# Delta net in a two-layer mixer block: decay columns spread by two rounded products, backward direction reversed by its reads

## The chip, the cores and the metric

The kernel runs on one core of a Trainium2 chip. The metric is the device time of one execution in microseconds (us); lower is better. TensorE (PE) does the matrix products, its weight loads are shown apart as PEld; VectorE (DVE), ScalarE (ACT) and GpSimd (POOL) do the elementwise work; SyncE (SP) issues most of the transfers.

## The reference

Two layers over 256 latent and 256 context tokens of width 1024. Each layer is a half-step SwiGLU, then four token mixers side by side (a convolution, a linear recurrence, a gated delta net in both directions, windowed attention), merged by sigmoid gates, an output product and a second SwiGLU. The change touches the delta net alone:

```python
def gdn_chunked(q, k, v, beta, g, s0):
    ...
    gc = jnp.cumsum(g, axis=-1)
    decay = jnp.exp(jnp.where(tril, gc[..., :, None] - gc[..., None, :], -jnp.inf))
    ...
def gdn_branch(qkv, qkv_c, z, z_c, a, a_c, b, b_c, p, ctx_out):
    for d in range(2):
        fl = _flip if d else _ident
        ...
        oc, s_ctx = gdn_direction(fl(qkv_c), ...)
        ol, _ = gdn_direction(fl(qkv), ..., s_ctx, *prm)
        o_lat.append(fl(ol))
        o_ctx.append(fl(oc))
    y = _gdn_out(o_lat[0] + o_lat[1], z, p['gdn_norm_g'])
    y_c = _gdn_out(o_ctx[0] + o_ctx[1], z_c, p['gdn_norm_g']) if ctx_out else None
```

There are 4 heads of 128 channels. The second layer needs no context output.

## The kernel before

Activations lie transposed in SBUF, weights stream in from HBM as `wr` or `raw`. The dense products are fp32 quantities split into two rounded (float32r) parts: ACT casts the high part (L123), DVE or POOL subtracts to get the low part (L124), and three products at L427, L428 and L429 add up high by high, high by low and low by high.

The delta net works on 16 chunks of 32 tokens in each direction; a partition row of 128 holds 4 heads by 32 tokens. For each layer its parts are:

- `gdn_scalars` computes the gates of both directions. The running sums come out of a product into `pg`, and L718 copies them to `gc` (a column of 128 values for each direction and chunk). L720 makes their negative `ngc`, L722 to L727 further factors. L817 turns two of these into tables.
- `gdn_decay` runs 8 times in a layer, each time for one direction and 4 chunks. L739 puts a constant mask (`capr`) into a bank of PSUM; L742 adds, chunk by chunk, the column of `gc` spread over 128 columns: the column is the stationary operand, broadcast, and the fp32 identity moves. An fp32 product is two instructions on PE, so a call has 8 of them at L742. ACT takes the exponential at L746 with `ngc` as the bias.
- the scan over the chunks: L923, L935 and L940 are its products, ACT (L942) and DVE (L943) finish the output of a step, and L945 stores every second step to `ospill` in DRAM. Both directions run in the same step; the backward one is stored in the order in which it is computed.
- `gdn_out` runs once for 128 tokens: 4 times in layer 0, twice in layer 1. It reads the backward part `o1`, the forward part `ot` (both L1009) and the gate `sz` (L1011); four fp32 products at L1014 with the constant `J` reverse the 32 tokens of each group of `o1`; L1016 adds, L1019 squares with a sum on ACT, L1021 and L1023 (a power on POOL) give the norm, L1025 applies it, L1028 transposes on PE, L1032 multiplies by the gate, and the split into rounded parts (L159, L161) gives the operand of the merges.

The streams of a layer (delta net, scan, `gdn_out`, merges, convolution, and the dense products that fill in between) are generators. A string per layer sets in which order they are stepped; the instruction scheduler then orders each engine's instructions by a simulated timeline, so that an edit can move instructions far from it. Each engine works off its instructions in the order that this gives, waiting on semaphores.

Of the kernel before, what the change touches and what calls it, by code (L numbers as in the profile page):

```python
# [12 lines left out]
F32 = mybir.dt.float32  # L13
F32R = mybir.dt.float32r
BF16 = mybir.dt.bfloat16
AF = mybir.ActivationFunctionType
ALU = mybir.AluOpType
P = 128
# [34 lines left out]
class Net:  # L53
# [609 lines left out]
    def gdn_scalars(self, l, H):  # L663
        nc = self.nc
# [32 lines left out]
        V.tensor_add(z3, A, self.vec[:, V_DT:V_DT + 2].unsqueeze(2).to_broadcast([P, 2, N_CH]))  # L697
        g = self.softplus(zz, 32, self.small(128, "gsp", 1))
        na = self.small(2, "na", 1)
# [17 lines left out]
        gc = self.small(64, "gc", 1)  # L717
        V.tensor_copy(gc, pg[:, :64])  # L718
        ngc = self.small(32, "ngc", 1)
        V.tensor_scalar(ngc, gc[:, :32], -1.0, None, op0=ALU.mult)  # L720
# [6 lines left out]
        nc.scalar.activation(kst, kst, AF.Exp)  # L727
        self.gs = dict(g=g, ngc=ngc, beta=be, gc=gc[:, :32], cd=cd.rearrange("p (n h) -> p n h", h=4), egc=eg, kst=kst)

# [5 lines left out]
    def gdn_decay(self, d, g, dec):  # L735
        nc = self.nc
        o = d * N_CH + 4 * g
        pr = self.ps("pg")
        nc.tensor.matmul(pr.rearrange("p (n c) -> p n c", n=4), self.identr,  # L739
                         self.capr.unsqueeze(1).to_broadcast([P, 4, P]), start=True, stop=False)  # L740
        for i in range(4):
            nc.tensor.matmul(pr[:, i * P:(i + 1) * P], self.gs["gc"][:, o + i:o + i + 1].to_broadcast([P, P]),  # L742
                             self.ident, start=False, stop=i == 3)
        for i in range(4):
            s = slice(i * P, (i + 1) * P)
            nc.scalar.activation(dec[:, s], pr[:, s], AF.Exp, bias=self.gs["ngc"][:, o + i:o + i + 1])  # L746
# [203 lines left out]
    def gdn_init(self):  # L950
        nc = self.nc
        dr = lambda n, s: self.dr.tile(s, F32, tag=n, bufs=1, name=n)
        self.gc_t = self.sb.tile([P, 776], F32, tag="R", bufs=2, name="gcst")
        nc.sync.dma_start(self.gc_t, self.t["gcst"])
        self.capr = self.sb.tile([P, P], F32R, tag="capr", bufs=1, name="capr")
        nc.scalar.copy(self.capr, self.gcst("cap"))
        self.gsp = dr("gsp", [8, P, 2, 3, 256])
        self.asp, self.ospill = (dr(n, [8, P, 2, 256]) for n in ("asp", "ospill"))
        self.ascr = dr("ascr", [2, P, 2048])
        self.rscr = dr("rscr", [P, 1024])  # L960
        self.szspill = dr("szspill", [P, 4, 512])
# [41 lines left out]
    def gdn_out(self, go, y):  # L1003
# [3 lines left out]
        tok = slice(go * P, (go + 1) * P)  # L1007
        for x, d, g in ((o1, 1, (1 - go) if go < 2 else (5 - go)), (ot, 0, go)):
            nc.sync.dma_start(x.rearrange("p (q c) -> p q c", q=2),  # L1009
                              self.ospill[2 * g:2 * g + 2, :, d].rearrange("q p c -> p q c"))  # L1010
        nc.sync.dma_start(sz.rearrange("p (h t) -> p h t", h=4), self.szspill[:, :, tok])  # L1011
        pj = self.ps("pg")
        for i in range(4):
            nc.tensor.matmul(pj[:, (3 - i) * P:(4 - i) * P], self.gcst("J"), o1[:, i * P:(i + 1) * P],  # L1014
                             start=True, stop=True)
        V.tensor_add(ot, pj, ot)  # L1016
        sq = self.small(4, "osq", 1)
        for i in range(4):
            nc.scalar.activation(pj[:, i * P:(i + 1) * P], ot[:, i * P:(i + 1) * P], AF.Square,  # L1019
                                 accum_out=sq[:, i:i + 1])  # L1020
# [600 lines left out]
```

## Time and profile before

| | |
|---|---|
| median of 3 runs | 2763.76 us (2760.72 to 2766.8) |
| profiled execution, its own time | 2763.57 us |
| its span on the core | 2761.8 us |
| granted TensorE clock, mean | 0.972 of full speed |
| PE busy | 2595.2 us (94%) |
| DVE busy | 1914.8 us (69%) |
| ACT busy | 1157.0 us (42%) |
| POOL busy | 716.5 us (26%) |

The span is what the profiler shows between the first and the last instruction; times such as "2445" are microseconds from its start. Layer 0's mixers lie at about 500 to 1060 us, layer 1's at about 2080 to 2470 us. A line like L742 is line 742 of the kernel before; the changed kernel's lines are some 3 or 4 higher from there on.

### The profile page before, as it was taken

Reading aid. Unit: us, or ns where it says so; the run is one execution under the profiler, and the core shown is the slowest. Engines: PE = TensorE matmul, PEld = TensorE weight load, DVE = VectorE, ACT = ScalarE, POOL = GpSimd, SP = SyncE. Lnnn points to the kernel's source line nnn. Section 1 sums busy time; section 2 is a strip of 40 time slices with the busy share of each in tenths; the row PEclk is TensorE's granted clock in tenths of the full one; section 3 lists DMA queues with packets and bytes.
Section 4 is the critical chain, followed back from the end, with each engine's and each line's share of the span. In section 5 each row is a group of like instructions: output and inputs, shape, how many; then the busy total and the mean of one; then the engine's idle time right before and its main releaser. Section 6 shows DMA issues by size and latency. Waiting matters only on the chain.

```text
span 2761.8 us, 38864 instructions
## 1 busy us (share of the span) xinstructions
PE 2595.2 (94%) x14534; PEld 2169.7 (79%) x14534; DVE 1914.8 (69%) x3261; ACT 1157.0 (42%) x2240; POOL 716.5 (26%) x497
## 2 busy tenths in 40 slices
PE   7999999998998999999999989999999988988998
PEld 4877778777777787878778887888897977877897
DVE  4795966678889734266979565748567899756455
ACT  3222245473454533353322353332444546545443
POOL 1323223223111334443233333332310011111221
PEclk9999999999999999999999999999999999999999
DMA  7554633245323434438865448965364764457353
GB/s 269 197 212 153 211 122 105 62 138 166 106 85 98 137 117 126 160 107 288 317 210 186 135 153 302 321 211 194 101 243 151 242 190 136 131 165 262 124 183 107
DMA packets 194779, 477.80 MB, mean 173 GB/s; under 512 B 32816, under 2 KB 72976, under 8 KB 192544
## 3 DMA queue, kind: packets, MB, share of 16 engines
q1 hardware_dynamic: 173216, 424.39, 46.6%
q10 hardware_dynamic: 15264, 30.95, 3.2%
q0 software_dynamic: 6112, 19.99, 1.8%
q8 instruction: 114, 1.87, 0.3%
q14 instruction: 73, 0.60, 0.1%
HBM read 401.82 MB, written 73.45 MB: 172 GB/s over the span
## 4 chain that ended last, share of the span: by engine, by line
PE 50%; DVE 13%; DMA 6%; ACT 4%; issue 3%; POOL 1%; SPq 0%; ACTq 0%; DVEq 0%; POOLq 0%
PE pm L427 13%; PE pm L429 13%; PE pm L428 13%; DMA C<-in_win_dram 2%; DVE C L1157 2%; DVE wl L124 2%; PE pg L923 1%; DVE junk L203 1%; DMA wr<-in_f_dram 1%; DVE lru L1099 1%; DMA wr<-in_wo_dram 1%; DVE G L913 1%; PE px L1297 1%; PE pg L428 1%; PE pg L427 1%
## 5 line engine op out<-in xcount | busy, mean ns | idle before, releaser
L427 PE MATMUL pm<-h,wh 128*128 128x512 f32 (+1 forms) x2512 | 897.5, 359 | 31.8 <-ACT h L159 9.8
L429 PE MATMUL pm<-h,wl 128*128 128x512 f32 (+1 forms) x2512 | 895.2, 357 | 10.0 <-DVE wl L124 9.9
L428 PE MATMUL pm<-h,wh 128*128 128x512 f32 (+1 forms) x2512 | 896.8, 357 | 5.6 <-POOL h L161 5.5
L123 ACT CAST wh<-wr 128x1024 fp32r<-128x1024 f32 x304 | 318.2, 1047 | 618.8 <-DMA wr<-in_f_dram 210.2
L427 PEld LDWEIGHTS pm<-h,wh 128*128 128x128 f32 x2512 | 480.8, 192 | 111.9 <-ACT h L159 12.1
L429 PEld LDWEIGHTS pm<-h,wl 128*128 128x128 f32 x2512 | 480.5, 191 | 88.2 <-DVE wl L124 15.1
L428 PEld LDWEIGHTS pm<-h,wh 128*128 128x128 f32 x2512 | 481.0, 192 | 77.9 <-POOL h L161 7.5
L124 POOL TENSOR_TENSOR wl<-wr,wh 128x1024 fp32r<-128x1024 f32 x108 | 279.8, 2591 | 605.6 <-ACT wh L123 593.9
L124 DVE TENSOR_TENSOR wl<-wr,wh 128x1024 fp32r<-128x1024 f32 x196 | 269.3, 1375 | 215.8 <-ACT wh L123 215.0
L203 DVE SCALAR_TENSOR_TENSOR junk<-wa,cb 128x1024 bf16<-128x1024 f32 x256 | 364.3, 1462 | 9.0 <-DMA wa<-in_adaw_dram 3.9
L161 POOL TENSOR_TENSOR F<-G,F 128x512 fp32r<-128x512 f32 (+1 forms) x94 | 139.1, 1479 | 356.4 <-ACT F L159 341.9
L1157 DVE SCALAR_TENSOR_TENSOR C<-C,vec 128x482 f32<-128x482 f32 (+29 forms) x240 | 162.7, 678 | 4.4 <-ACT C L1149 1.4
L427 PE MATMUL pm<-wh,F 128*128 128x512 f32 x368 | 144.4, 396 | 7.7 <-DVE G L441 3.9
L428 PE MATMUL pm<-wl,F 128*128 128x512 f32 x368 | 144.2, 392 | 0.0
L429 PE MATMUL pm<-wh,F 128*128 128x512 f32 x368 | 143.4, 392 | 0.0
L124 DVE TENSOR_TENSOR wl<-raw,wh 128x1024 fp32r<-128x1024 f32 x62 | 76.3, 1232 | 65.9 <-ACT wh L123 65.9
L140 DVE TENSOR_TENSOR T<-C,T 128x512 fp32r<-128x512 f32 x76 | 68.3, 902 | 68.1 <-ACT T L138 64.8
L919 ACT ACTIVATE wk<-wk,cd 128x128 f32<-128x128 f32 x224 | 75.2, 392 | 87.3 <-PE pg L940 49.2
L441 DVE TENSOR_TENSOR G<-G,pm 128x512 f32<-128x512 f32 (+1 forms) x93 | 54.4, 585 | 79.9 <-PE pm L429 76.5
L159 ACT CAST F<-G 128x512 fp32r<-128x512 f32 (+1 forms) x94 | 50.9, 541 | 135.4 <-DVE G L441 135.3
L123 ACT CAST wh<-raw 128x1024 fp32r<-128x1024 f32 x64 | 67.0, 1049 | 89.7 <-PE pm L428 42.7
L620 DVE SCALAR_TENSOR_TENSOR G<-pm,vec,G 128x506 f32<-128x506 f32 (+5 forms) x126 | 87.2, 692 | 21.9 <-ACT G L615 20.2
(408 smaller groups left out, 4399.9 us busy)
## 6 DMA issues: line engine op xcount, KB each, us to landing
wr<-in_f_dram SPq DMA_DIRECT2D x204, 512.0 KB, 4.3
wa<-in_adaw_dram SPq DMA_DIRECT2D x64, 1024.0 KB, 5.1
wr<-in_win_dram SPq DMA_DIRECT2D x94, 512.0 KB, 3.6
raw<-in_f_dram SPq DMA_DIRECT2D x30, 1024.0 KB, 5.0
C<-in_win_dram SPq DMA_DIRECT2D x76, 256.0 KB, 5.0
pre<-T ACTq DMA_DIRECT2D x76, 256.0 KB, 4.9
pre<-T POOLq DMA_DIRECT2D x76, 256.0 KB, 5.7
wl<-pre SPq DMA_DIRECT2D x36, 512.0 KB, 5.3
```

What stands on the lines that cost most here:

```text
L123: nc.scalar.copy(h, r)
L124: (nc.gpsimd if pool_lo else nc.vector).tensor_sub(l, r, h.bitcast(F32))
L140: nc.vector.tensor_sub(lo, raw, h.bitcast(F32))
L161: eng.tensor_sub(lo, src, hi.bitcast(F32))
L203: nc.vector.scalar_tensor_tensor(junk, w3[:, a], 1.0, self.cb[:, s], op0=ALU.mult, op1=ALU.mult, accum_out=self.modT[l][:, i + a, s:s + 1])
L427: nc.tensor.matmul(ps, wh, xh, start=first, stop=False)
L428: nc.tensor.matmul(ps, wh, xl, start=False, stop=False)
L429: nc.tensor.matmul(ps, wl, xh, start=False, stop=last)
L441: nc.vector.tensor_mul(hf[:, c], sg[:, c], pu[:, c])
L620: nc.vector.scalar_tensor_tensor(acc[:, :, d:], src[:, :, :n - d], w(j), acc[:, :, d:], op0=ALU.mult, op1=ALU.add)
L919: nc.scalar.activation(S(d, n + 1)[:, hc], S(d, n)[:, hc], AF.Copy, scale=gs["cd"][:, d * N_CH + n, h:h + 1])
L1157: V.scalar_tensor_tensor(o, x, w(j), o, op0=ALU.mult, op1=ALU.add)
```

## The change

In `gdn_scalars` two rounded columns are made from `gc`: `gcr[0]` is its rounded copy (ACT), `gcr[1]` the rounded rest (DVE). `gdn_decay` spreads both, with the rounded identity moving: eight rounded products for four fp32 ones. In `gdn_out` the backward part is read by four transfers, each of 32 tokens of 4 heads, with the rows of each group in reverse; the products with `J` are gone, the add reads `o1` from SBUF, and the squares are written there. A small workspace of `softplus` moves into the tile of constants.

```diff
-        g = self.softplus(zz, 32, self.small(128, "gsp", 1))
+        g = self.softplus(zz, 32, self.gc_t[:, 776:904])
...
         V.tensor_copy(gc, pg[:, :64])
+        gcr = [self.sb.tile([P, 32], F32R, tag=f"gcr{e}", bufs=1, name="gcr") for e in range(2)]
+        nc.scalar.copy(gcr[0], gc[:, :32])
+        V.tensor_sub(gcr[1], gc[:, :32], gcr[0].bitcast(F32))
...
         for i in range(4):
-            nc.tensor.matmul(pr[:, i * P:(i + 1) * P], self.gs["gc"][:, o + i:o + i + 1].to_broadcast([P, P]),
-                             self.ident, start=False, stop=i == 3)
+            for gc in self.gs["gcr"]:
+                nc.tensor.matmul(pr[:, i * P:(i + 1) * P], gc[:, o + i:o + i + 1].to_broadcast([P, P]),
+                                 self.identr, start=False, stop=i == 3 and gc is self.gs["gcr"][1])
...
-        self.gc_t = self.sb.tile([P, 776], F32, tag="R", bufs=2, name="gcst")
-        nc.sync.dma_start(self.gc_t, self.t["gcst"])
+        self.gc_t = self.sb.tile([P, 904], F32, tag="R", bufs=2, name="gcst")
+        nc.sync.dma_start(self.gc_t[:, :776], self.t["gcst"])
...
-        for x, d, g in ((o1, 1, (1 - go) if go < 2 else (5 - go)), (ot, 0, go)):
-            nc.sync.dma_start(x.rearrange("p (q c) -> p q c", q=2),
-                              self.ospill[2 * g:2 * g + 2, :, d].rearrange("q p c -> p q c"))
+        nc.sync.dma_start(ot.rearrange("p (q c) -> p q c", q=2),
+                          self.ospill[2 * go:2 * go + 2, :, 0].rearrange("q p c -> p q c"))
+        g = (1 - go) if go < 2 else (5 - go)
+        for i in range(4):
+            nc.sync.dma_start(o1[:, i * P:(i + 1) * P],
+                              self.ospill[2 * g + 1 - i // 2, :, 1, (1 - i % 2) * P:(2 - i % 2) * P]
+                              .rearrange("(h t) c -> h t c", h=4)[:, ::-1])
         nc.sync.dma_start(sz.rearrange("p (h t) -> p h t", h=4), self.szspill[:, :, tok])
-        pj = self.ps("pg")
-        for i in range(4):
-            nc.tensor.matmul(pj[:, (3 - i) * P:(4 - i) * P], self.gcst("J"), o1[:, i * P:(i + 1) * P],
-                             start=True, stop=True)
-        V.tensor_add(ot, pj, ot)
+        V.tensor_add(ot, o1, ot)
...
-            nc.scalar.activation(pj[:, i * P:(i + 1) * P], ot[:, i * P:(i + 1) * P], AF.Square,
+            nc.scalar.activation(o1[:, i * P:(i + 1) * P], ot[:, i * P:(i + 1) * P], AF.Square,
                                  accum_out=sq[:, i:i + 1])
```

The scheduler places the new and the old instructions as follows. First DVE in layer 0, at the end of `gdn_scalars`; `cv` and `G` are the convolution of the delta net's inputs, `mx` belongs to the attention. Before:

```order
L718 COPY gc_3824<-pg_3816 128x64 [waits PE_49]
L720 TENSOR_SCALAR ngc_3826<-gc_3824 128x32 [waits DVE_49]
L726 TENSOR_TENSOR kst_3832<-gc_3824 128x32
L658 SCALAR_TENSOR_TENSOR cv_3531<-G_3960,G_3955 128x16x32 [waits Activation_49]
L1264 TENSOR_REDUCE mx_4583<-px_4586 128x1 [waits PE_49]
L620 SCALAR_TENSOR_TENSOR G_3963<-px_3183,vec_3143,G_3963 128x2x253 [waits Activation_49,Pool_49]
L817 TENSOR_TENSOR gcst_3475<-egc_3830,gcst_3475 128x128 [waits Activation_49]
L817 TENSOR_TENSOR gcst_3475<-kst_3832,gcst_3475 128x128 [waits Activation_49]
```

The same place of the changed kernel:

```order
L718 COPY gc_3823<-pg_3815 128x64 [waits PE_49]
L723 TENSOR_SCALAR ngc_3829<-gc_3823 128x32 [waits DVE_49]
L729 TENSOR_TENSOR kst_3835<-gc_3823 128x32
L658 SCALAR_TENSOR_TENSOR cv_3531<-G_3995,G_3990 128x16x32 [waits Activation_49]
L1268 TENSOR_REDUCE mx_4618<-px_4621 128x1 [waits PE_49]
L620 SCALAR_TENSOR_TENSOR G_3998<-px_3183,vec_3143,G_3998 128x2x253 [waits Activation_49,Pool_49]
L721 TENSOR_TENSOR gcr_3826<-gc_3823,gcr_3825 128x32 [waits Activation_49]
L821 TENSOR_TENSOR gcst_3475<-egc_3833,gcst_3475 128x128 [waits Activation_49]
```

The subtraction that makes the low column (L721) stands behind the convolution step at L620.

Then PE at the end of layer 1's mixers, from the last product of the scan to the first merge; `pm` banks are dense products (24 in a group: 8 pieces of 3 products), `y` is the output of `gdn_out`. Before:

```order
L935 MATMUL pg_19934<-vn_19932,G_19549 128x128 [waits DVE_49]
L940 MATMUL pg_19934<-wk_18669,gt_19547 32x128 x4
...
L427 MATMUL pm_21035<-h_15873,wh_21031 128x256 [waits Activation_49]
...
L1014 MATMUL pg_20796<-G_20790,gcst_16524 128x128 [waits DMAHW2_49,PE_49]
L1014 MATMUL pg_20796<-G_20790,gcst_16524 128x128 x3
...
L429 MATMUL pm_21066<-h_15873,wl_21063 128x256
L1028 MATMUL pg_20811<-ident_63,G_20791 128x128 [waits DMAHW3_49,DVE_49,PE_49]
L1028 MATMUL pg_20811<-ident_63,G_20791 128x128 x3
L1014 MATMUL pg_20890<-G_20884,gcst_16524 128x128 [waits DMAHW5_49,PE_49]
L1014 MATMUL pg_20890<-G_20884,gcst_16524 128x128 x3
L1028 MATMUL pg_20905<-ident_63,G_20885 128x128 [waits DMAHW6_49,DVE_49,Activation_49]
L427 MATMUL pg_20986<-y_20822,wh_20918 128x256 [waits PE_49,Activation_49]
```

The changed kernel from its last scan product on:

```order
L939 MATMUL pg_19996<-vn_19994,G_19611 128x128 [waits DVE_49]
L944 MATMUL pg_19996<-wk_18731,gt_19609 32x128 x4
L427 MATMUL pm_20986<-h_15900,wh_20982 128x256 [waits Activation_49]
...
L427 MATMUL pm_21017<-h_15900,wh_21013 128x256 [waits Activation_49]
...
L427 MATMUL pm_21093<-h_15900,wh_21089 128x256 [waits Activation_49]
...
L427 MATMUL pm_21124<-h_15900,wh_21120 128x256 [waits Activation_49]
L428 MATMUL pm_21124<-h_15901,wh_21120 128x256
L1032 MATMUL pg_20871<-ident_63,G_20853 128x128 [waits DMAHW5_49,DVE_49,PE_49]
L1032 MATMUL pg_20871<-ident_63,G_20853 128x128 x3
...
L1032 MATMUL pg_20963<-ident_63,G_20945 128x128 [waits DMAHW4_49,DVE_49,PE_49]
L1032 MATMUL pg_20963<-ident_63,G_20945 128x128 x3
L427 MATMUL pg_21044<-y_20882,wh_20976 128x256 [waits PE_49,Activation_49]
```

Four groups of 24 dense products now stand between the last scan product and the merges, where there were 2 products left of one group and two groups more; the second transposes no longer have products of `gdn_out` ahead of them.

At the same place DVE's order in the changed kernel (only `gdn_out`'s own instructions):

```order
L1020 TENSOR_TENSOR G_20853<-G_20852,G_20853 128x512 [waits DMAHW6_49,DMAHW7_49,DMAHW2_49,DMAHW1_49]
L1025 TENSOR_SCALAR osq_20862<-osq_20862 128x4 [waits Activation_49]
L1029 TENSOR_TENSOR G_20853<-G_20853,orr_20868 128x512 [waits Pool_49]
L1020 TENSOR_TENSOR G_20945<-G_20944,G_20945 128x512 [waits DMAHW6_49,DMAHW5_49,DMAHW7_49,DMAHW4_49,DMAHW0_49]
...
L1036 SCALAR_TENSOR_TENSOR G_20852<-pg_20871,vec_16232,G_20854 128x128 [waits DMAHW3_49,PE_49]
```

The second call's add (the second L1020) stands directly behind the first call's L1029, and waits for transfers alone.

## Rows read from the trace of the kernel before

**Rows 1.** The page: busy time of each engine, share of the span, instructions.

```profile
PE 2595.2 (94%) x14534; PEld 2169.7 (79%) x14534; DVE 1914.8 (69%) x3261; ACT 1157.0 (42%) x2240; POOL 716.5 (26%) x497
```

**Rows 2.** Busy time by stretch: length, PE, PEld, DVE, ACT, POOL, clock, DMA.

```profile
524.00:531.00 7.00, 7.00 (x53) 6.42 (x52) 6.83 (x15) 5.76 (x19) 2.36 (x1) 1.00 0.24 75
531.00:540.00 9.00, 6.61 (x45) 5.42 (x44) 6.63 (x16) 9.00 (x36) 0.00 (x0) 1.00 0.01 2
960.00:1060.00 100.00, 98.00 (x477) 79.29 (x475) 47.98 (x82) 41.69 (x82) 40.53 (x26) 1.00 0.41 126
2084.00:2460.00 376.00, 337.98 (x2587) 295.64 (x2586) 304.93 (x688) 205.44 (x523) 36.56 (x32) 0.96 0.54 171
2445.00:2460.00 15.00, 7.12 (x52) 6.82 (x53) 8.29 (x17) 5.82 (x20) 2.04 (x2) 0.88 0.44 143
```

**Rows 3.** Instructions by line, PE and PEld: busy us, mean (or min/median/max) ns.

```profile
L742 PEld LDWEIGHTS pg<-ident,gc x128: 185/190/192, 524.4 to 2113.2; 128*128 128x128 f32 x128
...
L428 PEld LDWEIGHTS pm<-h,wh 128*128 128x128 f32 x2512 | 481.0, 192 | 77.9 <-POOL h L161 7.5
...
L1014 PE MATMUL pg<-G,gcst 128*128 128x128 f32 x48 | 6.9, 276 | 1.7 <-DMA G<-ospill 1.7
...
L389 PE MATMUL px<-T 128*128 128x2 f32 x32 | 3.9, 244 | 0.8 <-DVE T L386 0.8
```

**Rows 4.** Timeline of layer 0's decay columns: start us, us, what.

```profile
524.05 2.36 POOL L124 TENSOR_TENSOR wl<-wr,wh 128x1024 fp32r<-128x1024 f32 x1 [3.61 <-PE pg L739]
...
524.37 2.07 DVE L720 TENSOR_SCALAR ngc<-gc 128x32 f32<-128x32 f32 x1
...
524.51 1.95 PE L742 MATMUL pg<-ident,gc 128*128 128x128 f32 x16
...
526.71 3.19 ACT L746 ACTIVATE dec<-pg,ngc 128x128 f32<-128x128 f32 x12
...
527.40 0.73 DVE L620 SCALAR_TENSOR_TENSOR G<-px,vec,G 128x506 f32<-128x506 f32 x1
...
528.05 0.28 DVE L817 TENSOR_TENSOR gcst<-egc,gcst 128x128 f32<-128x128 f32 x1
```

**Rows 5.** The chain, 2430 to 2470 us: start us, us, what.

```profile
2437.44 0.40 PE pg L940 x8
...
2438.64 2.77 DMA ospill<-G
2441.43 3.53 DMA G<-ospill
...
2446.26 0.70 DVE G L1016
...
2448.98 1.03 POOL orr L1023
...
2458.37 1.08 PE pg L1028 x4
2459.45 0.21 PE pg L427
...
2463.26 0.12 PE pg L427
```

**Rows 6.** PE's waits, 2437 to 2463 us: total us, times, longest.

```profile
PE pg L1028 <- issue: 7.8, 2, 6.0
```

**Rows 7.** Timeline of SP's queue in layer 0: start us, us, what.

```profile
938.13 0.53 SPq L1011 DMA_DIRECT2D G<-szspill  x1
949.47 0.35 SPq L107 DMA_DIRECT2D wr<-in_prj_dram  x1
```

**Rows 8.** Timeline of SP's queue in layer 1.

```profile
2444.12 0.53 SPq L1011 DMA_DIRECT2D G<-szspill  x1
2451.89 0.34 SPq L107 DMA_DIRECT2D wr<-in_prj_dram  x1
```

**Rows 9.** The reading of `szspill` (L1011): issue to landing in us.

```profile
DMA to landing us min/median/max: 3.9/4.9/7.1
```

More of the change, by code (lines that the diff above doesn't have):

```diff
@@ L727, in gdn_scalars @@
         nc.scalar.activation(kst, kst, AF.Exp)
-        self.gs = dict(g=g, ngc=ngc, beta=be, gc=gc[:, :32], cd=cd.rearrange("p (n h) -> p n h", h=4), egc=eg, kst=kst)
+        self.gs = dict(g=g, ngc=ngc, beta=be, gcr=gcr, cd=cd.rearrange("p (n h) -> p n h", h=4), egc=eg, kst=kst)
     def gcst(self, n):
```

## The prediction

> **What bounds the kernel now.** I read the page's busy line first [rows 1]: TensorE is busy 94% of the span, DVE 69%, ACT 42%. Where PE is full, an instruction taken from it pays its whole length; where PE waits, only the chain that it waits for counts. So the next view was the busy time by stretch, at the three places that the change touches [rows 2].
>
> Place A, 524 to 540 us, holds the decay columns of layer 0: PE is full until 531 and then busy 6.61 of 9 us, while ACT is busy 9.00 of 9, so ACT's exponentials set the pace there. Place B, 960 to 1060 us, holds the four `gdn_out` calls of layer 0: PE is busy 98.00 of 100 us. Place C, 2445 to 2460 us, holds the two `gdn_out` calls of layer 1: PE is busy 7.12 of 15, in the hole at the end of the delta net's scan. The waits of PE show who makes the hole [rows 6]: from 2437 to 2463 us the transposes at L1028 wait 7.8 us. The chain there [rows 5] runs from the last scan product (L940) through the store of the scan's output, its reading back, the reversal by J at L1014, the add, squares, power and transposes to the first merge product at 2459.45.
>
> **The profiled execution** took 2763.57 us (span 2761.8), the median is 2763.76: they differ by 0.2 us, so no correction is needed. This kernel's measurement tells 0.2%, 5.5 us, from no change.
>
> **The decay products (L742 to L746).** Per call, four fp32 matmuls of two instructions each become eight rounded ones: 8 instructions before and after, 128 over both layers [rows 3]. Sixteen of them in a row take 1.95 us [rows 4]; less the last one's own length, 0.276 by the J products of the same form [rows 3], that is 1.674/15 = 0.112 us each. The column count does not set this: an instruction on 2 moving columns is 244 ns long, one on 128 columns 276 [rows 3]. A rounded product on 128 columns is not in the trace. The nearest rows are the rounded 256-column products of the merges, 0.12 us apart [rows 5], and the weight load of a rounded operand, 192 ns, as against 185 to 192 of the fp32 one [rows 3]. If columns alone set the pace, 128 of them take half of 0.12, 0.06; if the weight load does, 0.112; if a narrow rounded product pays like a whole fp32 one, 2 x 0.112 = 0.224. The weight loads are alike, so I take 0.112: **0 us** (low 128 x -0.052 = -6.7, high 128 x +0.112 = +14.3).
>
> The Trainium skill speaks for the low end: "TensorE: Matmul & The Clock Gate", section "Weight-path perf modes — Fast Weight Load (FWL) and DoubleRow", says that a load of 128 weights whose type isn't FP32 is automatically fast, about twice as quick when measured. The trace does not bear that out for this rounded type: 192 ns beside 190 in the median. By the rule the sum would be up to 6.7 us lower, by the row 0.
>
> **The two new tiles.** The high column is one ACT copy of 128x32 (some 0.2 us), the low one a DVE subtraction (0.28 at most, by L817 on four times the columns, [rows 4]). They matter by their place. On DVE of layer 0 the subtraction is not put behind L718 but after the 0.73 us convolution step at L620, in the place where the first L817 stood: 528.05 us [rows 4]. Before, the products needed only `gc` and began at 524.51; the first exponential began at 526.71. Now every call needs the low column. Queued behind it on PE, in order, are the remaining products of the calls, and ACT's exponentials wait for these; the subtraction ends near 528.3, products and semaphores take some 0.8, first exponential near 529.1, 2.4 later. Since ACT is the full engine up to 540, most of that stays; a little is won since products that PE would run later come forward into the gap. **+2.0 us** (0 to +3.0). Why DVE is so late there: L720, a column operation on 32 columns, takes 2.07 us beside POOL's 2.36 us subtraction, where the 128 columns of L817 take 0.28 without it [rows 4]. If POOL's stands elsewhere, the lateness is gone: that is the 0. In layer 1, 18 ready products stand in PE's order ahead of the first high column, 18 x 0.12 = 2.2 us of cover: **0** (±1).
>
> **J leaves (L1014).** 48 instructions [rows 3], 32 of them in place B, where PE is full: 32 x 0.112 = **-3.6 us**. The add at L1016 now reads SBUF for PSUM, and the squares write SBUF; DVE is busy 47.98 of 100 us and ACT 41.69 there [rows 2], which covers it; without cover it would be some tenths per call.
>
> **More transfers.** Each call issues six transfers for three. An issue costs SP some 0.53 us [rows 7], so 3 x 0.53 = 1.6 us per call. In layer 0 SP is through with the reads of two calls at 938.66 and issues nothing until 949.47 [rows 7]: 10.8 us cover the 3.2. In layer 1 the last issue ends at 2444.65 and the next is at 2451.89 [rows 8]: 7.2 us of cover. The reversed reads have rows of 512 bytes; the nearest row is the reading of `szspill`, the same row length, which lands in 3.9 to 7.1 us, 4.9 in the median [rows 9], as against 3.53 for the last reading of `ospill` [rows 5]. Only the two quarters out of the last-written block have to wait for the last store; the other two go early. **0**; a landing at the slow end, 7.1, instead of 3.53 would cost 3.6 once, in place C.
>
> **Place C.** Before, from L940's end at 2437.84 to the first merge at 2459.45 are 21.6 us [rows 5], under which stand some 50 dense products (50 x 0.12 = 6.0 us), J and the transposes. I lay the same chain out for the changed kernel, in us behind the last scan product. Before, the power of the first call ends at 2450.01, 12.2 behind it; J with its semaphore, from the landing at 2444.96 to the add at 2446.26, was 1.3 of that. So the power ends at 10.9 and the product by it (0.7, as the add of the same size) at 11.6, and the first transposes follow. The second call was worse off before: its J stood in PE's order behind the first transposes, and its own transposes began at 2458.37, 20.5 behind. Now its add needs no PE and stands on DVE directly behind the first call's product, at 11.6. From the add's start to the power's end took 3.75 us in the first call (2446.26 to 2450.01); with 0.7 for the product and some 0.5 for gaps the second transposes begin at 16.6, take 1.08, and the merges begin near 18.0.
>
> PE's order moves too: the last scan product now stands ahead of four groups of 24 dense products (96 x 0.12 = 11.5 us) instead of 50 (6.0). The interval would be 21.6 - 18.0 = 3.6 us shorter and hold 5.5 us more work that is done elsewhere now: -9.1, J's 16 instructions among it (16 x 0.112 = 1.8). But the 46 products brought in here are missing beside the last scan steps, which may stall there; between -1.8 (all lost) and -9.1 I count two thirds. **-6.0 us.** (PE's clock could add to it: 18 merge products ran at 0.21 instead of 0.12 us, up to 2463.26 [rows 5], 1.6 us, if PE, idle less, kept its full clock.)
>
> **Sum.** 0 + 2.0 + 0 - 3.6 + 0 - 6.0 = -7.6: 2763.57 - 7.6 = **2756.0 us**.
>
> **Rivals.**
> *Rounded loads are quick (R1).* The eight products take 0.06 each. Half of them are hidden in place A behind ACT, so some -3.4 more: 2752.6. For it: the columns are few. Against: equal weight loads. The skill's rule on fast loads, above, is this case. Chance 0.10.
>
> *The narrow rounded product is dear (R2, the other side).* Each of the 128 costs like a whole fp32 product, 0.224: +14.3, where the term stood at 0, less nothing since PE then paces place A: 2756.0 + 14.3 = 2770.3. For it: a rounded product is known here only at 256 columns and more. Against: its weight load is no longer than others. The gain is gone when each costs 7.6/128 = 0.059 more, at 0.171 us; above (7.6 + 5.5)/128 = 0.102 more, 0.214 us, the kernel is slower. Chance 0.10.
>
> *The scan only stalls elsewhere (R3).* The last scan steps come earlier in PE's order, but each still waits for DVE's and ACT's part, and with 46 fewer products between them PE waits there for what it gained in place C: -1.8 remains of -6.0, so 2760.2, within 0.2%. For it: the stalls of layer 1's mixers are 38 us (376 less 337.98, [rows 2]) and most sit in the scan. Chance 0.20.
>
> *The reversed reads land late (R4).* 3.6 us more in place C: 2759.6. For it: the spread in [rows 9]. Chance 0.07.
>
> *The rest of the order opens stalls (R5).* The scheduler places names anew all over the mixers; PE waits 38.0 us in 2084 to 2460 [rows 2]. Two fifths more there is +15: 2771. I found no place for it. Chance 0.10.
>
> **Numbers.** My forecast has 0.43, of which 0.36 lies below 2758.1 (faster) and 0.07 above it. Faster: 0.36 + 0.10 (R1) = 0.46. Same: 0.07 + 0.20 + 0.07 = 0.34. Slower: 0.10 + 0.10 = 0.20. The range reaches from 2749 (R1 with place C at -9.1: 2752.6 - 3.1 = 2749.5) to R2 and R5 at 2770; the likeliest case alone would be 2752 to 2760.
>
> **What the profile after would show.** Right: 128 rounded products 0.11 us apart; first exponential of layer 0 near 529, some 2.4 later than before relative to the products at L739; no L1014, and PE full in place B; in place C the hole smaller by some 5 us, with the first transposes about 11.7 us behind the last scan product and the merges about 18. Wrong: products 0.06 or 0.22 us apart (R1, R2); PE's waits at the scan's lines grown by 4 us or more (R3); reads of 64 KB landing over 6 us behind their issue and PE waiting for them (R4); a new wait of several us at a line that the diff doesn't touch (R5).

## The result and the profile after

The changed kernel takes 2779.9 us (median of 4 runs, 2776.9 to 2789.85), the kernel before 2764.57 beside it: a ratio of 1.006 [1.0044, 1.0076] (in brackets the 95% interval), so 0.6% slower; the medians lie 15.3 us apart. A second set of runs of the same file gave 1.0049 [1.0035, 1.0063]. Both sets lie above 2770, where the predicted range ended.

The profiled execution of the changed kernel took 2789.85 us (span 2788.0), 10 us over its median; what is read from it below was compared with the trace of the second set, which ran at its median (2779.44). Its busy line on the page, beside [rows 1]:

```profile
PE 2603.3 (93%) x14486; PEld 2175.3 (78%) x14486; DVE 1912.6 (69%) x3263; ACT 1155.4 (41%) x2242; POOL 718.1 (26%) x497
```

The 48 products of J are gone, and still PE is busy 8 us longer here; in the trace of the second set (2593.8) it is busy as long as before. A busy time that doesn't fall when instructions leave points at the clock.

**Where the time went.** Every kernel here has 11,064 dense products (L427 to L429), so the start of the n-th one marks the same amount of dense work done, whatever moved. The table gives, for a stretch between two such products, the length less the mean of two traces of the kernel before (which lie 0.2 to 1.2 us from their mean). It is worked out from the traces, in us; each figure is that of one trace, and a trace can lie some us beside its kernel's median.

| stretch, by product | mean of before | after | after, second set |
|---|---|---|---|
| 1800–2400, place A | 237.3 | +8.8 | +8.6 |
| 2700–3300, place B | 166.0 | +13.6 | +10.8 |
| 3900–4200, the FFN (feed-forward) behind layer 0's mixers | 56.9 | +2.7 | +1.9 |
| 4200–5000, the same FFN | 189.0 | +5.3 | +1.2 |
| 6000–7800, ahead of the mixers of layer 1 | 397.1 | −2.0 | −4.0 |
| 7800–9300, mixers of layer 1 | 416.3 | −3.5 | −3.3 |

**Place A**, the timeline of the changed kernel's decay columns, beside [rows 4] (start us, us, what; in brackets the idle time ahead of it and what ended that):

```profile
525.42 2.37 POOL L124 TENSOR_TENSOR wl<-wr,wh 128x1024 fp32r<-128x1024 f32 x1 [3.60 <-PE pg L742]
525.51 0.22 DVE L718 COPY gc<-pg 128x64 f32<-128x64 f32 x1
525.76 2.06 DVE L723 TENSOR_SCALAR ngc<-gc 128x32 f32<-128x32 f32 x1
...
526.79 0.21 ACT L720 CAST gcr<-gc 128x32 fp32r<-128x32 f32 x1
...
527.05 0.44 PE L746 MATMUL pg<-identr,gcr 128*128 128x128 f32 x2 [1.00 <-ACT gcr L720]
...
528.44 0.41 DVE L1268 TENSOR_REDUCE mx<-px 128x1 f32<-128x256 f32 x1
...
528.91 0.75 PE L1264 MATMUL px<-kv,q 128*128 128x256 f32 x2 [1.08 <-DVE mx L1268]
529.43 0.17 DVE L721 TENSOR_TENSOR gcr<-gc,gcr 128x32 fp32r<-128x32 f32 x1
...
529.66 4.74 PE L746 MATMUL pg<-identr,gcr 128*128 128x128 f32 x21
...
531.45 1.14 ACT L750 ACTIVATE dec<-pg,ngc 128x128 f32<-128x128 f32 x4 [3.27 <-PE pg L746]
```

The high column stands behind other work of ACT and is made 1.1 us after `gc`; PE waits 1.00 for it and then 1.08 for the attention's maximum. The low column comes at 529.43, 3.9 us behind L718. In the kernel before, the same place was:

```profile
524.12 0.22 DVE L718 COPY gc<-pg 128x64 f32<-128x64 f32 x1
...
527.06 0.41 DVE L1264 TENSOR_REDUCE mx<-px 128x1 f32<-128x256 f32 x1
```

The maximum begins 2.9 us behind the start of L718 in both kernels, so it is not later than it was. But before, PE had 24 products of the columns to run ahead of it; now three stand there. Before, the first product came 0.39 behind the start of L718 and the first exponential 2.59; now 1.54 and 5.94. And the products themselves grow slow: 21 of them in 4.74 us are 0.226 each. The busy time by stretch (length; PE, PEld, DVE, ACT, POOL; granted clock; DMA) says why:

```profile
528.00:530.00 2.00, 1.09 (x4) 0.64 (x4) 2.00 (x7) 0.18 (x1) 0.00 (x0) 0.86 0.51 117
530.00:532.00 2.00, 2.00 (x11) 2.00 (x11) 1.88 (x6) 0.55 (x3) 0.00 (x0) 0.50 0.36 145
532.00:542.00 10.00, 10.00 (x42) 9.24 (x42) 3.86 (x10) 7.90 (x28) 0.00 (x0) 0.50 0.01 2
542.00:544.00 2.00, 2.00 (x14) 1.96 (x14) 1.68 (x3) 2.00 (x9) 0.00 (x0) 0.73 0.00 0
```

From 530 to 542 us the clock is granted at 0.50, its lower level (1.2 of 2.4 GHz), after PE had waited in the microseconds before; [rows 2] had 1.00 in this place. PE is full where it had gaps, and ACT is no longer the full engine.

**Place B**, the timeline of the changed kernel at the first two `gdn_out` calls:

```profile
944.07 1.52 SPq L1012 DMA_DIRECT2D G<-ospill  x1
945.64 2.36 SPq L1016 DMA_DIRECT2D G<-ospill  x4
...
953.24 0.69 DVE L1020 TENSOR_TENSOR G<-G 128x512 f32<-128x512 f32 x1 [7.08 <-DMA G<-ospill]
953.44 1.26 SPq L1019 DMA_DIRECT2D G<-szspill  x1
953.97 0.31 ACT L1023 ACTIVATE G<-G 128x128 f32<-128x128 f32 x1 [4.15 <-DVE G L1020]
...
958.65 2.34 POOL L1116 TENSOR_TENSOR lru<-lru 128x1024 f32<-128x1024 f32 x1 [2.09 <-DVE lru L1114]
958.95 2.58 DVE L1020 TENSOR_TENSOR G<-G 128x512 f32<-128x512 f32 x1 [0.45 <-DMA G<-ospill]
...
961.62 0.31 ACT L1023 ACTIVATE G<-G 128x128 f32<-128x128 f32 x1 [4.11 <-POOL lru L1116]
...
962.80 1.03 ACT L123 CAST wh<-wr 128x1024 fp32r<-128x1024 f32 x1
...
963.88 0.80 PE L427 MATMUL pm<-h,wh 128*128 128x512 f32 x1 [8.17 <-ACT wh L123]
```

The add (L1020) stood at the head of DVE's queue for 7.08 us, waiting for the reversed reads; the squares stood twice at the head of ACT's, for 4.15 and 4.11 (the second row names POOL's L1116, but that ended at 960.99, and the second add at 961.53, just ahead of the square); behind them on ACT stood the cast of a weight (L123), for which PE waited 8.17. The first add now ran when 2,849 dense products had begun. In the kernel before, 3,004 had begun, and the reads had been issued from 50 us ahead of it on:

```profile
934.42 1.80 SPq L1009 DMA_DIRECT2D G<-ospill  x2
...
984.96 0.68 DVE L1016 TENSOR_TENSOR G<-pg,G 128x512 f32<-128x512 f32 x1
```

In the hole and just behind it the clock falls as well:

```profile
955.00:960.00 5.00, 0.71 (x17) 0.38 (x16) 2.51 (x4) 2.48 (x5) 2.37 (x2) 0.95 0.35 91
960.00:965.00 5.00, 1.12 (x3) 0.93 (x4) 4.47 (x6) 3.38 (x11) 2.75 (x2) 0.50 0.00 0
965.00:970.00 5.00, 5.00 (x14) 3.89 (x13) 5.00 (x7) 1.92 (x4) 4.53 (x3) 0.53 0.35 105
```

The second add took 2.58 us, the first 0.69. It ran beside POOL's 2.34 us at L1116 and ended half a microsecond behind it. The Trainium skill, "SBUF — State Buffer", section "SBUF: two separate sides", says that DVE and GpSimd share a pair of ports as an exclusive lock, which a DVE operation with two SBUF inputs takes against a GpSimd operation that reads SBUF. The row agrees: the add now reads `o1` from SBUF, where it had J's product in PSUM before.

**Place C**, the chain of the changed kernel, beside [rows 5]:

```profile
2458.11 0.35 PE pg L944 x8
...
2465.16 5.67 DMA ospill<-G
...
2475.07 5.33 DMA G<-ospill
...
2486.49 0.44 PE pg L1032 x4
```

From the scan's last product (ends 2458.46) to the end of the last transposes, where the merges begin, is 28.5 us, not the 18.0 of the prediction: the store begins 6.7 us behind the product, takes 5.67 instead of 2.77, and SP's issues take 4.2. On DVE three weight subtractions (L124) now stand between that product and the scan's last output (L947, from 2464.79). PE is covered better all the same: of the 7.8 us for which the transposes waited [rows 6], 0.6 are left. Its waits from 2456 to 2490 us:

```profile
PE pm L427 <- ACT wh L123: 3.9, 2, 2.1
PE pm L429 <- DVE wl L124: 2.9, 2, 2.2
PE pg L1032 <- issue: 0.6, 1, 0.6
```

### The profile page after: what moved, and what is told of

Read it like the earlier page. It is cut to its first block, busy times and chain, and to the rows that moved or that the text cites. A ratio compares the mean times of both kernels' runs of the same rounds, so it can differ in the third digit from the quotient of the medians.

```text
span 2788.0 us, 38788 instructions
## 1 busy us (share of the span) xinstructions
PE 2603.3 (93%) x14486; PEld 2175.3 (78%) x14486; DVE 1912.6 (69%) x3263; ACT 1155.4 (41%) x2242; POOL 718.1 (26%) x497
## 4 chain that ended last, share of the span: by engine, by line
PE 38%; DVE 6%; DMA 5%; issue 3%; ACT 3%; POOL 1%; SPq 0%; ACTq 0%; POOLq 0%; DVEq 0%
PE pm L428 10%; PE pm L429 10%; PE pm L427 10%; DMA C<-in_win_dram 3%; DVE junk L203 1%; DVE T L140 1%; PE px L429 1%; PE px L428 1%; PE px L427 1%; DVE wl L124 1%; PE pg L927 1%; PE px L1301 0%; POOL h L161 0%; ACT wh L123 0%; PE px L1264 0%
## 5 line engine op out<-in xcount | busy, mean ns | idle before, releaser
L427 PE MATMUL pm<-h,wh 128*128 128x512 f32 (+1 forms) x2512 | 901.2, 361 | 45.0 <-ACT wh L123 17.0
L429 PE MATMUL pm<-h,wl 128*128 128x512 f32 (+1 forms) x2512 | 898.7, 359 | 16.0 <-DVE wl L124 15.9
L123 ACT CAST wh<-wr 128x1024 fp32r<-128x1024 f32 x304 | 318.3, 1047 | 643.3 <-DMA wr<-in_f_dram 209.4
L427 PEld LDWEIGHTS pm<-h,wh 128*128 128x128 f32 x2512 | 484.1, 193 | 124.8 <-ACT wh L123 19.7
L429 PEld LDWEIGHTS pm<-h,wl 128*128 128x128 f32 x2512 | 484.6, 193 | 92.8 <-DVE wl L124 21.3
L124 POOL TENSOR_TENSOR wl<-wr,wh 128x1024 fp32r<-128x1024 f32 x108 | 277.7, 2571 | 604.1 <-ACT wh L123 517.8
L124 DVE TENSOR_TENSOR wl<-wr,wh 128x1024 fp32r<-128x1024 f32 x196 | 272.6, 1391 | 205.6 <-ACT wh L123 204.5
L203 DVE SCALAR_TENSOR_TENSOR junk<-wa,cb 128x1024 bf16<-128x1024 f32 x256 | 358.5, 1438 | 9.0 <-ACT cb L182 3.9
L161 POOL TENSOR_TENSOR F<-G,F 128x512 fp32r<-128x512 f32 (+1 forms) x94 | 137.0, 1458 | 368.8 <-ACT F L159 332.9
L427 PE MATMUL pm<-wh,F 128*128 128x512 f32 x368 | 143.6, 393 | 2.5 <-DVE M L574 2.5
L429 PE MATMUL pm<-wh,F 128*128 128x512 f32 x368 | 143.7, 393 | 0.0
L124 DVE TENSOR_TENSOR wl<-raw,wh 128x1024 fp32r<-128x1024 f32 x62 | 76.1, 1229 | 60.4 <-ACT wh L123 60.4
L159 ACT CAST F<-G 128x512 fp32r<-128x512 f32 (+1 forms) x94 | 50.9, 541 | 127.6 <-DVE G L441 127.5
L620 DVE SCALAR_TENSOR_TENSOR G<-pm,vec,G 128x506 f32<-128x506 f32 (+5 forms) x126 | 87.2, 692 | 23.8 <-ACT G L615 22.4
L123 ACT CAST wh<-raw 128x1024 fp32r<-128x1024 f32 x64 | 66.9, 1048 | 83.9 <-PE pm L428 39.3
```

Source lines behind the costliest of these rows:

```text
L123: nc.scalar.copy(h, r)
L124: (nc.gpsimd if pool_lo else nc.vector).tensor_sub(l, r, h.bitcast(F32))
L161: eng.tensor_sub(lo, src, hi.bitcast(F32))
L203: nc.vector.scalar_tensor_tensor(junk, w3[:, a], 1.0, self.cb[:, s], op0=ALU.mult, op1=ALU.mult, accum_out=self.modT[l][:, i + a, s:s + 1])
L427: nc.tensor.matmul(ps, wh, xh, start=first, stop=False)
L429: nc.tensor.matmul(ps, wl, xh, start=False, stop=last)
```

## Experiments

Ratios are to the kernel before, run beside it on the same chip, with their 95% intervals; stretches are those of the table above, and A, B are places A and B. Stretches come from one trace each.

**The changed kernel again** (no edit).

> The changed kernel once more, for a second trace. My theory is that the time is lost in layer 0 alone: some 10 us at the decay columns, where PE waits for the high and the low column and its granted clock is 0.50 for some 13 us behind it, and some 11 to 13 us at the four output calls, where the add on DVE and the squares on ACT wait for the reversed reads at the head of their queues and hold up the weight cast behind them. Then both holes stand in this trace too, the time is 2776 to 2790 us, and what differs from the first trace lies in the feed-forward stretches (up to 10 us). Rival: the holes are accidents of the first trace; then one of them is missing here and the time is below 2774.

Measured: 2779.41 us, 1.0049 [1.0035, 1.0063]. Both holes stand in this trace too; the two traces differ by 2.8 us at B and by 4.1 in the FFN (4200–5000).

**The decay part alone**: `gdn_scalars`, `gdn_decay` and the workspace as changed, `gdn_out` as before.

```diff
+        nc.scalar.copy(gcr[0], gc[:, :32])
+        V.tensor_sub(gcr[1], gc[:, :32], gcr[0].bitcast(F32))
...
+            for gc in self.gs["gcr"]:
```

> The rounded decay columns alone; the output calls with J are as before. Theory (late columns and the clock): +8 to +12 us, 2772 to 2776, all of it at the decay columns of layer 0, with PE waits of about 1 us for the ACT copy and about 1 us and more in front of the low column, and 0.50 granted behind them; the products are 0.11 us apart where the clock is 1.00 and 0.22 where it is 0.50. Rival (a narrow rounded product is dear by itself): the products are 0.22 us apart at full clock too, and layer 1 loses some 7 us as well. Rival (only the output calls lose): 2763, no change.

Measured: 2772.51, 1.0021 [1.0007, 1.0036]. Place A +8.5, place B +2.4, layer 1's mixers −4.0. So place A's loss is the decay part's, and layer 1's gain comes though J is still there. The FFN (3900–4200) has +5.0, which the expectation hadn't.

**The reversed reads alone**: no J, fp32 decays.

```diff
-        pj = self.ps("pg")
...
-        V.tensor_add(ot, pj, ot)
+        V.tensor_add(ot, o1, ot)
```

> The reversed reads alone, without J; the decay columns stay fp32. Theory (add and squares wait at the head of DVE and ACT for reads that land late): a PE hole of 6 to 9 us near the first output calls of layer 0 with 0.50 granted behind it, +8 to +12 us there, -2 to -4 in layer 1, so 2768 to 2774. Rival (my prediction's terms, the decay columns the only loss): -9 us, 2755. Rival (order elsewhere): the loss lies at lines of the scan or the convolution in layer 1.

Measured: 2775.32, 1.0036 [1.0022, 1.0051]. Place A −1.4, place B +10.9, the FFN (3900–4200) +6.9, layer 1 −2.3. The two parts add up: 0.21 + 0.36 = 0.57%, between the 0.49 and 0.60 of the whole. That is luck in part: together the halves have +11.9 us in the FFN (3900–4200), the whole kernel 1.9 to 2.7.

**The high column on DVE** (the decay part alone, and).

```diff
-        nc.scalar.copy(gcr[0], gc[:, :32])
+        V.tensor_copy(gcr[0], gc[:, :32])
```

> As the decay columns alone, but both rounded columns are made by DVE directly behind the running sums; the low one then stands ahead of the convolution step instead of behind it. Theory (lateness opens the holes and these drop the clock): PE waits once, some 2 us, instead of twice; if that keeps the clock at 1.00 the time is 2764 to 2767, if the clock falls all the same it is 2769 to 2773. Rival (the columns' place does not matter): as the decay columns alone, 2772 to 2776.

Measured: 2764.29, 0.9995 [0.9981, 1.0009]; place A +2.1. Neither expectation held as written: the copy now took the 2.05 us beside POOL, and the clock fell too, but the stretch lost a quarter of what it had lost (the second fence is busy time by stretch, as above).

```profile
526.91 2.35 POOL L124 TENSOR_TENSOR wl<-wr,wh 128x1024 fp32r<-128x1024 f32 x1 [3.62 <-PE pg L742]
...
527.24 2.05 DVE L720 CAST gcr<-gc 128x32 fp32r<-128x32 f32 x1
```

```profile
536.00:540.00 4.00, 4.00 (x18) 3.81 (x19) 1.55 (x4) 3.15 (x13) 0.00 (x0) 0.50 0.02 4
```

So the low clock alone doesn't price place A. Layer 1 stands at +0.4, and 6000–7800, which holds nothing of the edit, at −7.0.

**Both columns from PSUM by DVE**, ahead of the copy to `gc` (the decay part alone, and).

```diff
-        V.tensor_copy(gc, pg[:, :64])
-        nc.scalar.copy(gcr[0], gc[:, :32])
-        V.tensor_sub(gcr[1], gc[:, :32], gcr[0].bitcast(F32))
+        V.tensor_copy(gcr[0], pg[:, :32])
+        V.tensor_sub(gcr[1], pg[:, :32], gcr[0].bitcast(F32))
+        V.tensor_copy(gc, pg[:, :64])
```

> The decay columns alone, both made by DVE, and both read from PSUM instead of from gc in SBUF, ahead of the copy to gc. My theory is now that the long column operation (2.06 us) is a DVE operation on SBUF alone that stands still until POOL's subtraction beside it ends; one that reads PSUM does not (the copy to gc takes 0.22 us beside the same POOL operation). Then both columns take about 0.2 us each, PE waits less than 0.8 us for the first one, the granted clock stays 1.00 in the whole stage, and the time is 2761 to 2766, the loss of the stage (+7) gone. Rival (any DVE operation there is slow, or the clock falls for another reason than PE's waits): the first column still takes 2 us, or the clock falls to 0.50 all the same, and the stage loses 3 us or more.

Measured: 2777.82, 1.0042 [1.0027, 1.0057], but place A −1.1: its loss is gone. The timeline and the stretch of this kernel:

```profile
527.98 2.37 POOL L124 TENSOR_TENSOR wl<-wr,wh 128x1024 fp32r<-128x1024 f32 x1 [3.61 <-PE pg L742]
528.07 0.18 DVE L719 CAST gcr<-pg 128x32 fp32r<-128x32 f32 x1
528.29 0.19 DVE L720 TENSOR_TENSOR gcr<-pg,gcr 128x32 fp32r<-128x32 f32 x1
528.31 2.04 PE L746 MATMUL pg<-identr,gcr 128*128 128x128 f32 x16
528.64 1.75 DVE L723 TENSOR_SCALAR ngc<-gc 128x32 f32<-128x32 f32 x1
```

```profile
531.00:544.00 13.00, 9.89 (x71) 8.75 (x70) 10.46 (x26) 12.83 (x49) 0.00 (x0) 1.00 0.11 42
```

From PSUM the columns take 0.18 and 0.19 us beside the same POOL subtraction that holds `ngc`, read from SBUF, for 1.75. The products run 16 in 2.04 us, the clock stays at 1.00, ACT is full again as in [rows 2]. The theory of the stage held; the time did not. Its trace is 15.9 us longer than the two of the kernel before in the mean, all of it elsewhere: FFN (3900–4200) +6.3, layer 1 +6.3, 6000–7800 −5.6. A third cause was needed.

**Four reads, J kept** (the kernel before; `o1` read by four forward transfers of 64 KB).

```diff
+        for i in range(4):
+            nc.sync.dma_start(o1[:, i * P:(i + 1) * P],
+                              self.ospill[2 * g + i // 2, :, 1, i % 2 * P:(i % 2 + 1) * P])
```

> The kernel before, but the backward part is read by four transfers in forward order, with J kept: the transfers of the change without what it takes from PE. Theory (the loss comes from DVE and ACT waiting for the reads at the head of their queues, since the add no longer stands behind PE): the add keeps its place behind J, no hole in layer 0, 2762 to 2766, although the reads are issued and land as late as in the changed kernel (5 us behind the last issue). Rival (the small transfers themselves are the loss, through SP's queue or through the memory): +8 to +11 us as in the reversed reads alone.

Measured: 2768.64, 1.0011 [1.0000, 1.0023]; place B +0.6. The time lies 2.6 us above the expected range, with +3.1 ahead of product 1800, which the edit doesn't touch. The count of transfers alone is not place B's loss.

**The add placed later** (the reversed reads alone; in layer 0 the add may be issued only behind the convolution norm's product of the same tokens).

```diff
+        with self.tc.issue_after(self.cn[go]) if self.l == 0 else nullcontext():
+            V.tensor_add(ot, o1, ot)
...
+            self.cn[t] = V.tensor_mul(v3, pt.rearrange("p (i t) -> p i t", i=4), g4).ins
```

> The reversed reads alone, without J, but in layer 0 the add is queued on DVE behind the convolution's multiplication of the same tile, about the place that it had with J (row 1099 of DVE's order instead of 1071). Theory: the hole of 8 us and the low clock behind it are gone, J's 32 instructions are saved there (-3.6), and layer 1 keeps -2 to -3: 2757 to 2762. Rival (transfers): still +8 to +11.

Measured: 2774.01, 1.0033 [1.0019, 1.0047]; the trace is of a run of 2779.99. The hole is gone and the gain did not come. Its longest wait of PE from 940 to 1000 us is now

```profile
PE pm L427 <- ACT M L1335: 2.1, 1, 2.1
```

and between products 2850 and 2875, where the reversed reads alone had +9.45 us, it has 0.0: the place of the add made the hole. Between products 2925 and 3250 it is 2.0 us quicker than before, of the 3.6 that J was to give. It has +1.8 between 2875 and 2925, and +6 at the stretch's end, where one wait was 0.8 us before:

```profile
PE px L1176 <- DMA T<-cspill: 2.7, 1, 2.7
```

So place B as a whole still stands at +6.1, and the FFN (3900–4200) at +7.6.

**Both mended** (the changed kernel with the columns from PSUM and the add later).

> The whole change with both mends: columns from PSUM and the add queued later in layer 0. If both theories hold, nothing of the loss is left and J is saved: 2755 to 2762, faster than the kernel before by 0.1 to 0.3%. If only one holds, 2768 to 2774.

Measured: 2779.68, 1.0049 [1.0035, 1.0063], though place A is at +1.5 and place B at +1.4; the FFN (3900–4200) is at +7.4. The trace is of a run of 2773.65, so some 6 us of the median's loss don't show in it.

**The kernel before again.**

> The kernel before once more, for a second trace of it: 2760 to 2768 us. My theory is that the first trace was unlucky in the feed-forward stretch of layer 1 (all other traces are 2 to 9 us quicker there), so this one is some 5 us quicker there and slower elsewhere; the stretches of the mixers agree within 2 us. If they do not, the differences by stretch that I read off single traces are worth less.

Measured: 2765.85, 1.0 [0.9991, 1.0008]: 0.2% is well told from nothing. Its mixers agree with the first trace within 2 us, as expected; 6000–7800 is 2.4 us shorter, not 5.

**The kernel before with late transposes.** In the FFN behind layer 0's mixers the eight transposes at L303 that a generator leaves for later (`finish`) stand in PE's order among 72 dense products: six ahead of them and two behind in the kernel before, all eight behind in the five kernels so far whose FFN was 5.0 to 7.6 us longer (3900–4200). Here the eight are put behind them, with nothing else touched.

```diff
-                        self.finish()
+                        with self.tc.issue_after(self.mm) if (l, f) == (0, 1) else nullcontext():
+                            self.finish()
```

> The kernel before, with nothing of the change: only the eight transposes at L303 in the second feed-forward step of layer 0 are queued on PE behind the 72 products that follow them, where all changed kernels but the one with DVE columns and the one that keeps J have them by the scheduler's own choice (the kernel before has six of them ahead). Theory: this reordering, far from the edit, is a part of the loss: PE waits some 3 us and then 1.5 us for the columns made of the transposes, and the stretch takes 6 to 9 us more: 2769 to 2774. Rival (only what the edit touches costs time): 2762 to 2767.

Measured: 2771.71, 1.0018 [1.0008, 1.0028], as the theory said; the FFN (3900–4200) +8.1. The transposes of the kernel before,

```profile
1240.37 0.82 PE L303 MATMUL pg<-ident,T 128*128 128x128 f32 x6
...
1249.56 0.38 PE L303 MATMUL pg<-ident,T 128*128 128x128 f32 x2
```

of this one, its first two waits of PE from 1215 to 1275 us, and below them the longest of the kernel before:

```profile
1251.60 1.04 PE L303 MATMUL pg<-ident,T 128*128 128x128 f32 x8
```

```profile
PE pm L427 <- ACT h L159: 3.8, 2, 3.0
PE pm L428 <- POOL h L161: 2.7, 2, 1.8
```

```profile
PE pm L428 <- POOL h L161: 2.1, 1, 2.1
```

L159 and L161 make the operand of the next products out of these transposes. An order that the diff doesn't touch is worth 0.18% alone.

**Both mended, transposes earlier** (behind 24 of the 72 products) and **held ahead** of all 72. The first edit, then the second:

```diff
-                            if i == 0:
-                                self.finish(1)
+                            if i < (2 if (l, f) == (0, 1) else 1):
+                                self.finish(1 + i)
...
+                                if (l, f, i, e) == (0, 1, 1, 0):
+                                    self.finish()
```

> The whole change with both mends and these transposes stepped earlier in the feed-forward step: they stand behind 24 of the 72 products, 48 products (5.8 us) are left to cover the columns. Theory: 6 to 8 us less than the mended kernel with late transposes (2779.7), so 2771 to 2774, and no wait over 1 us behind L303 in that stretch. Rival: no difference.

> The whole change with both mends, and all eight transposes of that feed-forward step queued ahead of the 72 products (the kernel before has six ahead and two behind). Theory: nothing is left of the loss there (-7 against the mended kernel with late transposes, 2 less than with 24 products ahead of them); the time is 2763 to 2767, within 0.1% of the kernel before. If it is below 2760, the change pays once its order is held. Rival (the gain of the last run was chance): 2772 or more.

Measured: 2767.51, 1.0004 [0.9991, 1.0016], and 2759.07, 0.9991 [0.998, 1.0002]; the FFN (3900–4200) +1.7 and +1.3. Both are quicker than their ranges. From the mended kernel to the one with the order held the traces differ by 6.1 us there, by 4.8 in 4200–5000 and by 3.2 in 6000–7800; only the first is where the transposes stand.

**The kernel before, and the changed one, with the transposes held ahead** (the same edit in each).

> The kernel before with only the held transposes of the last run (all eight ahead of the 72 products). If this holding alone is worth what the mended change had over the kernel before (6 us), this is 2757 to 2761 and the change itself pays nothing; if it is 2762 to 2767, the mended change is better by itself, through J's 48 products.

> The changed kernel with only the held transposes, none of the mends at the columns and the add. Theory (columns +8.7, output calls +12.2, layer 1 -3.4, and -4 to -6 for the feed-forward step that the holding gave the mended kernel): 2770 to 2778, slower than the kernel before by 0.2 to 0.5%. Rival (the loss is mostly the order of the feed-forward step): 2760 to 2766.

Measured: 2755.52, 0.9969 [0.9959, 0.998], and 2772.93, 1.003 [1.0018, 1.0041]. With that order made equal the change still costs 1.003/0.9969, 0.6%; A stands at +8.5 and B at +10.8. The mended kernel with the same order has 0.9991: the mends take back 0.39 of the 0.61%, and 0.22% remain (the intervals touch at 0.998). It came out below 2760, but the first of these two is the quickest kernel here, so the change pays in no run, mended or not. Only 1.6 and 1.7 of that kernel's gain lie in the FFN's two stretches; 6.7 lie in 6000–7800, where the kernel before waits 5.5 us between 1690 and 1800 us,

```profile
PE pm L427 <- DVE M L574: 3.0, 2, 2.1
PE pm L427 <- DVE G L441: 1.7, 1, 1.7
PE pm L427 <- ACT G L439: 0.8, 1, 0.8
```

and this one 0.4. How the transposes move these waits was not followed, and all kernels with any part of the change, most of them without the held order, stand at −1.1 to −7.0 in that stretch.

## Why the prediction was wrong

The stretches of the two traces of the changed kernel give, in the mean, A +8.7, B +12.2, the FFN +2.3 and +3.3, 6000–7800 −3.0, layer 1 −3.4: together +20, as their spans do (+25.2 and +14.8, mean 20.0). The first of the two is a run 10 us above its median; the medians differ by 15. By the prediction's own terms:

**The decay products, 0 us: right.** 16 rounded products take 2.04 us, as against 1.95 of the fp32 ones [rows 4]. Their weight loads have a minimum and a median of 185 and 192 ns, beside 185 and 190 of [rows 3]:

```profile
L746 PEld LDWEIGHTS pg<-identr,gcr x128: 185/192/337, 527.0 to 2145.2; 128*128 128x128 f32 x128
```

R1 (0.06 each) and R2 (0.224 each) both fall. The 0.226 of place A is the lower clock, not the dear product: eight of them, in 1.00 us from 543.19, ran quick again. In layer 1 PE waits for no column, the 0 there was right too.

**The late low column, +2.0 us: the mechanism was right, the term mis-sized at +8.7.** The lateness was read off DVE's order alone. It missed that the high column waits on ACT, that PE's own queue then waits for the attention, and that PE, idle in between, loses its clock for 12 us. The first exponential came 3.4 us later behind L718 than before, not 2.4. Columns taken from PSUM undo it (−1.1 with the decay part alone, +1.5 with both mends). How much of the 8.7 is clock and how much is lateness stays open: with the copy on DVE the clock fell as well, at a cost of 2.1.

**J leaves, −3.6 us, and more transfers, 0: these are the steps that failed, on the sentence that DVE's 47.98 busy of 100 us "covers it".** A share of busy time says nothing of who stands at the head of the queue. J on PE had kept the add late in DVE's order; without it the scheduler put the add about 30 places earlier on DVE (27 in the traces), in front of its data, and ACT's squares and a weight's cast queued behind. SP's 10.8 us of slack was no cover either. The six transfers of the first two calls took it 4.2 us before (934.42 to 938.66), the twelve of the change 10.6 (944.07 to 954.70). That is within the slack, but an add at the head of its queue waits for the landing, not for a free queue. The four reads with J kept (+0.6) and the later add (the hole gone) show that it was the place, not the transfers. Of the −3.6, 2.0 came through between products 2925 and 3250 once the hole was gone (2.7 with both mends), but over the whole stretch no kernel without J was quicker than before. The "some tenths per call" for the add's second operand in SBUF were too few as well: the second add took 2.58 us, 1.9 more than the first. Whether quicker reads would have closed the hole with the add in front was not run.

**Place C, −6.0 us: not borne out.** Layer 1's mixers gained 3.4, but the chain there is 28.5 us, not 18.0, and the decay part with J kept gained 4.0. Three kernels with J and two rounded columns range from −4.0 to +6.3 there (the decay part, with DVE columns +0.4, from PSUM +6.3). The hole at the transposes did close (7.8 to 0.6 us), and R3's sign did not come: PE waits 7.0 us for the scan's `vn` (DVE, L911), as against 6.6 before. So the sign agrees and the reason isn't shown; what decides that stretch is open.

**R5, "I found no place for it":** its sign, a new wait of several us at a line that the diff doesn't touch, is PE's 8.17 us for L123 in place B, and another place was the FFN of layer 0, with the transposes 0.18% when moved alone. It lost 5.0 to 7.6 us in the half-changed and mended kernels whose eight transposes stand behind, which is a part of why mending A and B alone didn't bring the time back. In the changed kernel itself seven stand ahead and one behind, so its own 2.3 there, and the 3.3 after it, have no shown cause.

The workspace of `softplus` was not run by itself.

## What to carry to other kernels

An operation that looks like pure cost may be what keeps its successor late in a queue: when it goes, ask where the scheduler will now put the successor, when its data comes, and who stands behind it. Where a clock can fall, price a wait of PE by what follows it too (though a stretch at half clock lost 8.5 us in one kernel and 2.1 in another), and read the head of each queue instead of the busy share. And when half-changes don't add up, compare two traces at equal amounts of work: order that moved far from the edit shows there, and can be tested alone.

## What the runs showed of the hardware

- A 128x32 column operation of DVE from SBUF beside POOL's 2.37 us subtraction took 2.06 and 2.05 us, from PSUM 0.18 and 0.19.
- An fp32 add of 128x512 with both inputs in SBUF took 2.58 us beside POOL's work and 0.69 without.
- Rounded products of one broadcast column came 0.11 us apart in the median at full clock, as the instructions of the fp32 ones did, and took 0.226 each (21 in 4.74 us) at the granted clock of 0.50, which lasted from 530 to 542 us although PE was full from 530 on.
- The issues of the 24 reads of 64 KB with rows in reverse held SP 0.51 to 1.02 us each, 0.54 in the median; forward reads of the same size (four reads, J kept) 0.32 to 1.25, 0.43 in the median.
